# Sixty-eight elementwise instructions of a three-layer network move from GpSimd to VectorE

## The chip, the cores and the metric

The kernel runs on one core of one Trainium2 chip. A core has a matrix engine (TensorE, PE in the profile; its weight loads are PEld), and three engines for elementwise work: VectorE (DVE), ScalarE (ACT) and GpSimd (POOL). SyncE (SP) only issues DMAs here. Each engine works off its own queue of instructions in order and waits for the others by semaphores. The metric is device time in microseconds (us); lower is better.

## What the kernel must compute

The reference takes 256 tokens of width 1024 through three layers, all in float32. Every layer adds a mixer and then a feed-forward part to the residual `x`, each behind an RMS norm whose shift, scale and gate come from a conditioning vector. In its core:

```python
# layer 0: forgetting attention and gated linear attention side by side, then SwiGLU (d_ff 2816)
x = x + g * even_mixer(rmsnorm(x, w) * (1 + sc) + sh, ...)
x = x + g * ((silu(h @ w_gate) * (h @ w_up)) @ w_down)
# layer 1: S5 state space, then a mixture of 8 experts, 2 of them for each token
a = exp(lam_re * dt) * (cos(lam_im * dt) + i sin(lam_im * dt))     # 64 groups x 64 states
y = gelu(C . scan(a, B u) + d_skip * u);  y = (y * sigmoid(y @ w_glu)) @ w_o
x = x + g * sum_e gates[e] * swiglu(h, expert e)
# layer 2: differential attention and RWKV from one input, merged, then PEER
g_a, g_b = split(sigmoid(z_gate))
x = x + g * ((g_a * (o_a @ w_branch_a) + g_b * (o_b @ w_branch_b)) @ w_out)
x = x + g * peer_ffn(...)                                          # 16384 single-row experts
```

## The kernel before

Activations lie transposed on the chip, as eight tiles `x[:, k]` of 128 channels by 256 tokens. Nearly every product is made of float32 operands that are **split** into a high and a low part (`split`, L443 to L447): ScalarE casts the operand to the high part (L445, `...h`), then a subtraction leaves the low part (L446, `...l`), and TensorE forms high x high, low x high and high x low (L421, L422, L423). Weights stream in from HBM: `wpair` (L454 on) loads a block on SP's queue (`w<-...`, L462) and splits it in pieces of 128x512 (`w2882h`, `w2882l` and so on). The block's buffer is free for SP's next load only when both halves of the split are done. `split` and `wpair` take an engine for the subtraction; without one it is VectorE.

The rows of `mods` (L317 to L341) are the conditioning of later layers, and are computed in the shade of earlier ones: 1 MB blocks `wm` are loaded on GpSimd's queue (L328) into two buffers, multiplied on TensorE (`mod<-wm`, L331), copied (`modrow`, L333), transposed (L336) and added to a bias (L339, L341).

Nobody writes the order of the work by hand. The program is built from Python generators, and a scheduler of the tile framework, which simulates a timeline while it builds, lays down the order on each engine. An edit therefore also shifts neighbours.

The places that matter here, in order of time:

- **S5 tables** (`s5_tables`, run as a generator from `layer0_ffn`). While layer 0's feed-forward part goes through its eleven blocks of 256 hidden columns (`gp0` to `gp10`; `gu` and `ga` are its products), powers of the state matrix are built by doubling. `cmul` (L766 to L773) is six tensor_tensor instructions, for 2, 4, ... up to 128 powers. For the last two doublings it is called with GpSimd:

```python
self.cmul(nc.gpsimd if i > 4 else v, tb[:, :, 0, n:2 * n], tb[:, :, 1, n:2 * n], ...
```

- **S5 stage** (`layer1_mix`): `ms`, the sum of squares of the norm (L379), follows on TensorE when `sq` (L378, ScalarE) has squared `x`; then `h2`, then the products `u`. The step over the states (`L910` to `L932`) has one product, `p4` at L919, on GpSimd before and after.
- **Sums of squares**: `route_begin.part` (L974, for the router), `ctx_norm` (L1321, for the context) and `layer2_mix` (L1383) square eight tiles and add them on GpSimd, seven or six additions each.
- **Experts' input** (`route`, L1059): four pieces of 128x512 are split, `hth` on ScalarE and `htl` on GpSimd, while VectorE works out each token's two experts. The one-hot matrix `oh` (L1098) ends that and releases TensorE's `xs` (L425).
- **Merge** (`merge`, L1910 on): while RWKV's last head pairs still run (`chain`, with `R`, `U`, `UV`, `S`, `Y` at L1743 to L1791), the first branch's weights `w_ba` go through a ring of tiles (`ring0h`, `ring0l`, `ringMA`, ...) with the subtraction on GpSimd, and the gate's half sums 0.5 z + 0.5 (`sigmoid`, L1924, tile `sg`) are made there as well; z is already the tanh.

Of the kernel before, what the change touches and what calls it, by code (L numbers as in the profile page):

```python
# [12 lines left out]
OP = mybir.AluOpType  # L13
# [5 lines left out]
KT = 8  # L19
# [230 lines left out]
class K:  # L250
# [524 lines left out]
    def s5_tables(self, p):  # L775
        nc, tc, A = self.nc, self.tc, self.A
        v = nc.vector
# [32 lines left out]
        with tc.tile_pool(name="s5pre2", bufs=1) as q:  # L810
            bs = q.tile([128, 2, 32, 16], F32, tag="bs", name="bs")
            cs = q.tile([128, 2, 32, 16], F32, name="cs")
            nc.gpsimd.dma_start(bs, A["s5_bs"])
            nc.gpsimd.dma_start(cs, A["s5_cs"])
            dte = q.tile([128, 32], F32, name="dts")
            nc.scalar.activation(dte, self.pvec("s5_dt"), AF.Exp)
            mag, co, si, fr, fi, t0, t1 = self.s5_a(q, self.pvec("s5_lr"), self.pvec("s5_li"), dte, 32, "st")
            v.tensor_mul(self.s5m, mag, mag)

            def bk(a, n=16):  # L820
                return a.rearrange("p (t o) -> p t o", o=1).to_broadcast([128, 32, n])

            b2 = q.tile([128, 2, 32, 16], F32, name="bb2")
            tt = q.tile([128, 32, 64], F32, tag="big", name="tt16")[:, :, :16]
            self.cmul(v, b2[:, 0], b2[:, 1], bk(fr), bk(fi), bs[:, 0], bs[:, 1], tt)
            ar, ai = q.tile([128, 32], F32, name="ar"), q.tile([128, 32], F32, name="ai")
            v.tensor_mul(ar, mag, co)
            v.tensor_mul(ai, mag, si)
            yield
            ca = q.tile([128, 2, 32, 16], F32, tag="bs", name="ca")  # L830
            self.cmul(v, ca[:, 0], ca[:, 1], bk(ar), bk(ai), cs[:, 0], cs[:, 1], tt)
            npar = q.tile([128, 2], F32, name="npar")
            v.tensor_scalar(npar, par64, -1.0, None, op0=OP.mult)
            bx = q.tile([128, 2, 32, 32], F32, tag="big", name="bx")
            for j in range(2):
                for dst, src, m in ((self.s5c[:, 0], cs[:, 0], par64), (self.s5c[:, 1], cs[:, 1], npar), (self.s5c[:, 2], ca[:, 0], par64),
                                    (self.s5c[:, 3], ca[:, 1], npar), (bx[:, 0], b2[:, 0], par64), (bx[:, 1], b2[:, 1], npar)):
                    v.tensor_scalar(dst[:, :, 16 * j:16 * j + 16], src, m[:, j:j + 1], None, op0=OP.mult)
            yield
            self.bank = "m"  # L840
            ps = self.psum("k0")
            for t8 in range(8):
                for r in range(4):
                    i = 4 * t8 + r
                    for m in range(2):
                        nc.tensor.matmul(ps[32 * r:32 * r + 32, 16 * t8:16 * t8 + 16], bx[:, m, i], cs[:, m, i], start=m == 0, stop=m == 1)
            k0 = q.tile([128, 8, 16], F32, name="k0")
            v.tensor_copy(k0, ps[:, :128].rearrange("p (t k) -> p t k", t=8))
            self.bank = "f"
            g16 = self.pvec("grp16")  # L850
            for t8 in range(8):
                v.tensor_mul(self.s5k[:, t8].rearrange("p (g k) -> p g k", g=8), k0[:, t8:t8 + 1].to_broadcast([128, 8, 16]),
                             g16.rearrange("p (g o) -> p g o", o=1).to_broadcast([128, 8, 16]))
            yield

            tb = self.s5t
            pw = q.tile([128, 7, 2, 32], F32, name="pw")
            self.cmul(v, pw[:, 0, 0], pw[:, 0, 1], co, si, co, si, t0)
            for i in range(6):
                self.cmul(v, pw[:, i + 1, 0], pw[:, i + 1, 1], pw[:, i, 0], pw[:, i, 1], pw[:, i, 0], pw[:, i, 1], t0)  # L860
            v.memset(tb[:, :, 0, 0:1], 1.0)
            v.memset(tb[:, :, 1, 0:1], 0.0)
            tmp = q.tile([128, 32, 64], F32, tag="big", name="tmp64")
            for i in range(7):
                n = 1 << i
                self.cmul(nc.gpsimd if i > 4 else v, tb[:, :, 0, n:2 * n], tb[:, :, 1, n:2 * n], tb[:, :, 0, 0:n], tb[:, :, 1, 0:n],
                          bk(pw[:, i, 0], n), bk(pw[:, i, 1], n), tmp[:, :, :n])
                if i > 3:
                    yield
# [83 lines left out]
    def route_begin(self):  # L953

        nc, v, mod = self.nc, self.nc.vector, self.mod
        sc = self.moe_sc = self.modscale("o_norm_ffn", mod[:, 80:88], "sc3")
        rt = self.pvec("router").rearrange("p (k e) -> p k e", k=8)
        rw = self.P.tile([128, KT, 8], F32, name="rw")
        v.tensor_mul(rw, rt, sc.rearrange("p (k o) -> p k o", o=1).to_broadcast([128, KT, 8]))
        ps = self.psum("rc")  # L960
        for k in range(KT):
            nc.tensor.matmul(ps[:, :8], mod[:, 72 + k:73 + k].to_broadcast([128, 128]), rt[:, k], start=k == 0, stop=k == KT - 1)
        rc = self.P.tile([128, 8], F32, name="rc")
        v.tensor_copy(rc, ps[:, :8])
        ps = self.psum("lg")
        xt = [[self.psum("xt") for _ in range(2)] for _ in range(2)]
        self.routed = ps, xt, rc
        sqs = []

        def part(k):  # L970
            sq = self.nt.tile([128, T], F32, tag="sq", name=f"rsq{k}", bufs=4)
            nc.scalar.activation(sq, self.x[:, k], AF.Square)
            if 0 < k < 7:
                nc.gpsimd.tensor_add(sq, sq, sqs[-1])  # L974
            sqs.append(sq)
            for t in range(2):
                xk = self.x[:, k, 128 * t:128 * t + 128]
                nc.tensor.matmul(ps[:, 16 * t:16 * t + 8], xk, rw[:, k], start=k + t == 0, stop=k == KT - 1, skip_group_check=True)
                if k >= 6:
                    nc.tensor.matmul(ps[:, 16 * t + 8:16 * t + 9], sq[:, 128 * t:128 * t + 128], self.ones_d[:, 0:1], start=False, stop=k == KT - 1, skip_group_check=True)  # L980
                nc.tensor.transpose(xt[t][k // 4][:, 128 * (k % 4):128 * (k % 4) + 128], xk, self.ident)

        return part

    def route(self, p, q, sc, sh, ht):
# [67 lines left out]
        for t in range(2):  # L1053
            for j in range(2):
                xp = xt[t][j]
                o = ht[:, t, 512 * j:512 * j + 512]
                hn = q.tile([128, 512], F32, name=f"hn{t}{j}")
                nc.scalar.activation(hn, xp, AF.Copy, scale=rs[:, t])
                self.split(hn, o, nc.gpsimd)  # L1059
        for t in range(2):  # L1060
            x, o = xf[:, t], sel[:, t]
            v.tensor_sub(x[:, 8:9], mx[:, t, 1:2], mx[:, t, 0:1])
# [239 lines left out]
    def ctx_norm(self):  # L1302
# [14 lines left out]
        for k in range(KT):  # L1317
            t = load(k, "a")
            nc.scalar.activation(t, t, AF.Square)
            if k:  # L1320
                nc.gpsimd.tensor_add(t, t, before)  # L1321
            before = t
        nc.tensor.matmul(ps[:, :T], self.ones_d, t, start=True, stop=True)
        r = self.rstd(ps[:, :T])
# [17 lines left out]
    def layer2_mix(self):  # L1342
        nc, tc, A, mod = self.nc, self.tc, self.A, self.mod
        m2 = mod[:, 96:144]
        with ExitStack() as c:
# [11 lines left out]
            with ExitStack() as c2:  # L1357
# [3 lines left out]
                with ExitStack() as c3:  # L1361
# [14 lines left out]
                    for k in range(KT):  # L1376
                        a = sq[:, KT + k % 2]
                        if k < 2:
                            v.tensor_scalar(a, sq[:, k], gs[:, 0, k:k + 1], None, op0=OP.mult)
                        else:  # L1380
                            v.scalar_tensor_tensor(a, sq[:, k], gs[:, 0, k:k + 1], a, op0=OP.mult, op1=OP.add)
                        if k:
                            nc.gpsimd.tensor_add(sq[:, KT + 2], sq[:, k], sq[:, KT + 2 if k > 1 else 0])  # L1383
                    for j in range(2):
                        nc.tensor.matmul(ps[0][:, :T], self.ones_d, sq[:, KT + j], start=j == 0, stop=j == 1)
                    self.scaled(self.x, self.rstd(ps[0][:, :T], eps=gs[:, 2, 0:1]), gs[:, 1], m2[:, 0:8], h2[:, :, T:])
# [523 lines left out]
    def merge(self, c, sz, oa, ob, h2, gate, chain):  # L1910
# [10 lines left out]

        def sigmoid(i):
            t = load(sz, i, "sg")
            nc.gpsimd.tensor_scalar(t, t, 0.5, 0.5, op0=OP.mult, op1=OP.add)  # L1924
            return t


# [13 lines left out]
        for b, wo in enumerate((A["w_ba"], A["w_bb"])):  # L1941
            for s in range(4):
                self.bank = "d" if b == 0 else ("a", "d", "ki")[s % 3]
                ws = self.wpair(wo[s], nc.gpsimd if b == 0 else None)
                for i, ps in enumerate(self.wT2("br", ws, h2[:, :, T * b:T * b + T]), 2 * s):
                    sg = sigmoid(KT * b + i)
                    v.tensor_mul(sg, ps[:, :T], sg)
                    if b == 0:
                        nc.sync.dma_start(ma[:, i], sg)
                    else:  # L1950
                        v.tensor_add(sg, sg, load(ma, i, "ma"))
                        self.split(sg, h2[:, i, :T])
# [287 lines left out]
```

## Time and profile before

| | |
|---|---|
| time, median of 3 runs | 3490.37 us (3477.37 to 3495.87) |
| the profiled execution | 3489.14 us, its span 3487.4 us |
| PE, PEld busy | 3207.4 us, 2648.6 us |
| DVE busy | 2309.6 us in 4717 instructions |
| ACT busy | 1710.9 us in 3107 |
| POOL busy | 467.2 us in 478 |

The profiled execution stands 1.7 us above its span and 1.2 us below the median. Busy time is summed over the whole span. "Granted clock" (PEclk) is the share of TensorE's full speed in a stretch. In a row of a timeline the first number is the start, the second how long it took (of several in a row: from the start of the first to the end of the last), and the brackets at the end tell how long the engine had idled before it and what ended that.

### The profile page before, as it was taken

What the parts mean: (1) busy time and instruction counts of PE and PEld (TensorE: products, weight loads), DVE (VectorE), ACT (ScalarE), POOL (GpSimd) and SP (SyncE); (2) the same over time, 40 slices, a digit from 0 to 9 for tenths busy, and PEclk for the clock granted to TensorE, in tenths of its full rate; (3) what the DMA queues carried; (4) which work ended last, traced back from release to release, by engine and by line L of the source; (5) the groups of instructions that cost most, each with busy time, mean ns of one, the idle gap of its engine ahead of it and who ended that gap; (6) DMA issues with size and microseconds to landing.
All of it is one profiled execution on the core that took longest, in us unless ns stands there. A gap on an engine that the chain in (4) does not pass through costs nothing. (4 is left out here: it accounts for less than half of the span.)

```text
span 3487.4 us, 67773 instructions
## 1 busy us (share of the span) xinstructions
PE 3207.4 (92%) x26800; PEld 2648.6 (76%) x26800; DVE 2309.6 (66%) x4717; ACT 1710.9 (49%) x3107; POOL 467.2 (13%) x478
## 2 busy tenths in 40 slices
PE   6989979989999999978899999899879989999999
PEld 4869967766668888746677677667779989988888
DVE  3568858753449999746766666566357767756665
ACT  4445423442226666514544544454436658755554
POOL 0000232200000000010000000000208853410000
PEclk8999988889999999988989888889789999999999
DMA  7666574478798999962111111111435545566775
GB/s 291 237 225 229 200 255 147 125 282 319 321 372 327 337 338 339 356 264 78 45 31 45 45 45 40 45 44 47 141 123 191 159 141 173 176 197 202 231 228 163
DMA packets 162435, 658.51 MB, mean 189 GB/s; under 512 B 18216, under 2 KB 37304, under 8 KB 118208
## 3 DMA queue, kind: packets, MB, share of 16 engines
q1 hardware_dynamic: 145344, 572.33, 46.6%
q0 software_dynamic: 16768, 81.80, 6.9%
q8 instruction: 212, 3.47, 0.4%
q14 instruction: 111, 0.91, 0.1%
HBM read 634.26 MB, written 19.79 MB: 188 GB/s over the span
## 5 line engine op out<-in xcount | busy, mean ns | idle before, releaser
L428 PE MATMUL mg<-mg,xs 128*64 128x256 f32 x1408 | 185.0, 386 | 3.7 <-ACT xf L1101 3.7
L1248 ACT ACTIVATE msg<-mg 128x128 f32<-128x128 f32 (+1 forms) x154 | 42.1, 273 | 260.3 <-PE mg L428 191.2
L428 PEld LDWEIGHTS mg<-mg,xs 128*64 128x64 f32 x1408 | 106.2, 138 | 68.1 <-issue 15.8
L331 PE MATMUL mod<-wm,c 128*32 128x256 f32 x1152 | 100.2, 452 | 50.0 <-DMA wm<-mods 45.5
L1363 POOL DMA_DIRECT2D h2h<-hch x1 | 1.0, 960 | 821.6 <-DVE squares L1372 821.6
L331 PEld LDWEIGHTS mod<-wm,c 128*32 128x32 f32 x1152 | 37.7, 123 | 87.7 <-DMA wm<-mods 44.4
L1814 POOL MEMSET X<- 128x272 f32 x8 | 3.0, 378 | 753.6 <-DVE UV L1754 217.9
L1249 DVE TENSOR_TENSOR msg<-msg,mg 128x128 f32<-128x128 f32 (+1 forms) x154 | 43.4, 282 | 76.4 <-ACT msg L1248 75.9
L328 POOL DMA_DIRECT2D wm<-mods x64 | 34.6, 541 | 386.2 <-PE mod L331 374.5
L2024 POOL TENSOR_SCALAR oh<-iota,idx 128x128 f32<-128x128 f32 x44 | 58.3, 1324 | 146.1 <-PE G L2034 146.1
L2027 ACT ACTIVATE oh<-oh,idx 128x128 f32<-128x128 f32 x212 | 69.1, 393 | 6.4 <-DVE oh L2019 6.4
L2019 DVE TENSOR_TENSOR oh<-iota,idx 128x1024 f32<-128x1024 f32 x53 | 67.6, 1278 | 0.0
L2034 PE MATMUL G<-oh 128*128 128x128 f32 x512 | 62.5, 275 | 0.0
L1152 DVE COPY mgt<-mg 128x128 f32<-128x128 f32 x44 | 12.8, 290 | 75.0 <-PE mg L1145 74.8
L367 DVE RECIPROCAL rs<-rs 128x512 f32<-128x512 f32 (+1 forms) x16 | 44.0, 2752 | 27.7 <-ACT rs L366 27.6
L2034 PEld LDWEIGHTS G<-oh 128*128 128x128 f32 x512 | 60.1, 192 | 0.0
L428 PE MATMUL ya<-md,mgt 128*64 128x512 f32 x176 | 55.1, 604 | 4.2 <-DVE mgt L1152 4.0
L2067 POOL DMA_DIRECT2D a<-ad x32 | 17.3, 542 | 284.9 <-DVE ap48l L446 127.1
L428 PE MATMUL yb<-md,mgt 128*64 128x512 f32 x176 | 54.0, 592 | 0.0
L2039 ACT COPY Gate<-G 128x288 f32<-128x288 f32 x64 | 43.3, 678 | 20.4 <-DVE acts L2038 20.4
L1760 PEld LDWEIGHTS S<-UV,BKt 128*64 128x64 f32 x448 | 22.3, 150 | 37.3 <-issue 13.8
L928 PE MATMUL y<-st,s5c 128*32 128x128 f32 x256 | 43.7, 320 | 6.5 <-DVE st L920 6.5
(11890 smaller groups left out, 12677.0 us busy)
## 6 DMA issues: line engine op xcount, KB each, us to landing
mg<-m_gu SPq DMA_DIRECT2D x176, 1024.0 KB, 7.8
md<-m_dn SPq DMA_DIRECT2D x88, 1024.0 KB, 8.0
wm<-mods POOLq DMA_DIRECT2D x64, 1024.0 KB, 6.1
w<-u SPq DMA_DIRECT2D x128, 512.0 KB, 3.7
w<-v SPq DMA_DIRECT2D x128, 512.0 KB, 4.2
w<-w_in SPq DMA_DIRECT2D x132, 256.0 KB, 2.7
w<-e_gu SPq DMA_DIRECT2D x44, 512.0 KB, 4.4
w<-e_in SPq DMA_DIRECT2D x24, 512.0 KB, 4.8
```

Of the source, the lines that this page charges most:

```text
L328: (nc.gpsimd if later else nc.sync).dma_start(ws, self.A["mods"][g, kp].rearrange("p j k c -> p (j k) c"))
L331: nc.tensor.matmul(ps[32 * j:32 * j + 32, :256], c[:, 2 * kp + k, :], ws[:, 2 * j + k, :], start=kp + k == 0, stop=kp + k == 4)
L367: nc.vector.reciprocal(t[:, :n], t[:, :n])
L428: mm(ps, w, h, start=start, stop=stop, **kw)
L928: nc.tensor.matmul(py[o, 128 * j:128 * j + 128], self.s5c[:, ci + m, i0 + r], st[:, r, m, off:off + 128], start=False, stop=m == 1, skip_g ...
L1248: nc.scalar.activation(sg[:rows], ps[:rows, :128], AF.Silu)
L1249: v.tensor_mul(sg[:rows], sg[:rows], ps[:rows, 128:256])
L2019: v_.tensor_tensor(o, iota.rearrange("p (a b i) -> p a b i", a=1, b=1).to_broadcast([128, 2, 4, 128]), idx[:, 0:2, 4 * t4:4 * t4 + 4].rear ...
L2024: nc.gpsimd.tensor_scalar(o[:, 0, t], iota, i1, w, op0=OP.is_equal, op1=OP.mult)
L2027: nc.scalar.activation(o[:, 0, t], o[:, 0, t], AF.Copy, scale=w)
L2034: nc.tensor.matmul(ps[:, 128 * t:128 * t + 128], o[:, 1, t], o[:, 0, t], start=True, stop=True)
L2039: nc.scalar.copy(G[0][:, :, ts].rearrange("p i t -> p t i"), pv[:, :, HF:120])
```

## The change

Seven calls lose their GpSimd argument or engine. Every instruction stays, with the same operands; 68 of them change their engine: 12 of the tables, 6 + 7 + 7 additions of squares, 4 subtractions of the experts' input, 16 subtractions and 16 half sums of the merge.

```diff
@@ s5_tables
-                self.cmul(nc.gpsimd if i > 4 else v, tb[:, :, 0, n:2 * n], tb[:, :, 1, n:2 * n], tb[:, :, 0, 0:n], tb[:, :, 1, 0:n],
+                self.cmul(v, tb[:, :, 0, n:2 * n], tb[:, :, 1, n:2 * n], tb[:, :, 0, 0:n], tb[:, :, 1, 0:n],
@@ route_begin.part
-                nc.gpsimd.tensor_add(sq, sq, sqs[-1])
+                nc.vector.tensor_add(sq, sq, sqs[-1])
@@ route
-                self.split(hn, o, nc.gpsimd)
+                self.split(hn, o)
@@ ctx_norm
-                nc.gpsimd.tensor_add(t, t, before)
+                nc.vector.tensor_add(t, t, before)
@@ layer2_mix
-                            nc.gpsimd.tensor_add(sq[:, KT + 2], sq[:, k], sq[:, KT + 2 if k > 1 else 0])
+                            v.tensor_add(sq[:, KT + 2], sq[:, k], sq[:, KT + 2 if k > 1 else 0])
@@ merge.sigmoid
-            nc.gpsimd.tensor_scalar(t, t, 0.5, 0.5, op0=OP.mult, op1=OP.add)
+            v.tensor_scalar(t, t, 0.5, 0.5, op0=OP.mult, op1=OP.add)
@@ merge
-                ws = self.wpair(wo[s], nc.gpsimd if b == 0 else None)
+                ws = self.wpair(wo[s])
```

On VectorE, in layer 0's feed-forward part around `gp8`, the table products (`s5t`, `tmp`) now stand among the splits of the weights (`w2872l` and so on, 128x512 each) and of the hidden columns (`gp8l`); `g` is the gated product:

```order
 L446 TENSOR_TENSOR w2880l<-w_4783,w2880h 128x512
+L770 TENSOR_TENSOR s5t<-s5t,tmp_4622 128x32x32
 L446 TENSOR_TENSOR w2882l<-w_4783,w2882h 128x512
 L446 TENSOR_TENSOR w2910l<-w_4851,w2910h 128x512
+L725 TENSOR_TENSOR g_4700<-gu_4721,sg_4770 128x256
+L772 TENSOR_TENSOR tmp_4622<-s5t,pw 128x32x32
+L768 TENSOR_TENSOR s5t<-s5t,pw 128x32x64
+L771 TENSOR_TENSOR s5t<-s5t,pw 128x32x64
 L446 TENSOR_TENSOR w2911l<-w_4851,w2911h 128x512
 L446 TENSOR_TENSOR w2920l<-w_4861,w2920h 128x512
-L725 TENSOR_TENSOR g_4700<-gu_4721,sg_4770 128x256
 L446 TENSOR_TENSOR gp8l<-g_4700,gp8h 128x256
```

Three products of 1024 and 2048 columns now lie between the splits, and `g` moves up ahead of them. In all, the twelve table instructions are spread from `gp7` to `gp9`.

On TensorE, behind layer 0's feed-forward part and ahead of the S5 stage, `mod<-wm` matmuls (a row for each 1 MB block `wm`) stand between the last `ga`, the norm's `ms` and the first `u`:

```order
 L423 MATMUL ga_2253<-gp10h,w3221l 128x256
-L331 MATMUL mod_5197<-wm_5208,c_90 32x256 x8
-L331 MATMUL mod_5197<-wm_5218,c_90 32x256 x8
 L331 MATMUL mod_5197<-wm_5228,c_90 32x256 x8
 L336 MATMUL mod_5197<-c_ident,modrow_5238 128x128 x2
-L331 MATMUL mod_6064<-wm_6065,c_90 32x256 x8
 L379 MATMUL ms_5496<-sq_0_5497,ones_d 128x256
 L379 MATMUL ms_5496<-sq_1_5500,ones_d 128x256
 L379 MATMUL ms_5496<-sq_2_5503,ones_d 128x256
 L379 MATMUL ms_5496<-sq_3_5506,ones_d 128x256
-L331 MATMUL mod_6064<-wm_6075,c_90 32x256 x8
+L331 MATMUL mod_6064<-wm_6065,c_90 32x256 x8
```

Of the seven blocks that stood between the last `ga` and the first `u`, four are left (`wm_5228`, `wm_6065`, `wm_6075`, `wm_6085`); `wm_5208` and `wm_5218` stand earlier, among `gu` and `ga`, and `wm_6095` with its `modrow` stands later, in the S5 stage's loop.

On ScalarE, in the merge, the casts of the ring and RWKV's `UV` of the last step of a head pair (`U_25329`) change places:

```order
 L445 CAST ring1h<-w_26623 128x512
+L445 CAST ring2h<-w_26627 128x512
+L445 CAST ring3h<-w_26631 128x512
 L1753 ACTIVATE UV_25103<-U_25329 64x128
-L445 CAST ring2h<-w_26627 128x512
 L1777 COPY y_25102<-Y_25336 128x2x64
 L1896 ACTIVATE TT_25458<-p_25611 16x16x16 x2
-L445 CAST ring3h<-w_26631 128x512
```

`UV` stood ahead of two casts that wait for a load, and now stands behind both.

## Rows read from the trace of the kernel before

**Rows 1.** The page: busy time of each engine, and one costly group.

```profile
PE 3207.4 (92%) x26800; PEld 2648.6 (76%) x26800; DVE 2309.6 (66%) x4717; ACT 1710.9 (49%) x3107; POOL 467.2 (13%) x478
...
L2019 DVE TENSOR_TENSOR oh<-iota,idx 128x1024 f32<-128x1024 f32 x53 | 67.6, 1278 | 0.0
```

**Rows 2.** Stretches: length, then busy time (instructions) of each engine, granted clock, DMA.

```profile
400.00:416.00 16.00, 16.00 (x162) 13.51 (x162) 14.72 (x45) 5.14 (x10) 2.11 (x4) 1.00 0.79 278
416.00:474.00 58.00, 41.88 (x344) 37.65 (x342) 48.46 (x36) 16.41 (x31) 40.54 (x16) 0.88 0.59 202
484.00:505.00 21.00, 21.00 (x201) 18.48 (x197) 11.69 (x26) 8.87 (x17) 2.11 (x4) 1.00 0.92 327
505.00:532.00 27.00, 16.01 (x130) 7.67 (x122) 6.33 (x13) 7.39 (x16) 3.17 (x6) 0.71 0.81 287
541.00:550.00 9.00, 8.91 (x75) 8.71 (x74) 4.45 (x6) 6.41 (x18) 4.12 (x7) 1.00 0.69 213
690.00:715.00 25.00, 24.13 (x204) 23.68 (x203) 9.15 (x18) 7.72 (x16) 4.62 (x6) 0.98 0.14 32
```

**Rows 3.** TensorE's waits from 416 to 480 us.

```profile
PE ga L421 <- ACT gp8h L445: 8.3, 1, 8.3
PE ga L422 <- DVE gp8l L446: 3.3, 1, 3.3
```

**Rows 4.** Timeline of GpSimd in the tables.

```profile
429.91 4.07 POOL L768 TENSOR_TENSOR s5t<-s5t,pw 128x2048 f32<-128x2048 f32 x1
...
437.96 0.60 POOL L328 DMA_DIRECT2D wm<-mods  x1
```

**Rows 5.** Timeline of VectorE ahead of the tables and in them.

```profile
405.83 0.42 DVE L771 TENSOR_TENSOR s5t<-s5t,pw 128x256 f32<-128x256 f32 x1
...
415.04 0.69 DVE L446 TENSOR_TENSOR w2832l<-w,w2832h 128x512 fp32r<-128x512 f32 x1
...
416.57 2.30 DVE L446 TENSOR_TENSOR w2840l<-w,w2840h 128x512 fp32r<-128x512 f32 x1
...
430.42 4.11 DVE L446 TENSOR_TENSOR w2882l<-w,w2882h 128x512 fp32r<-128x512 f32 x1
...
469.71 3.89 DVE L446 TENSOR_TENSOR gp9l<-g,gp9h 128x256 fp32r<-128x256 f32 x1 [0.47 <-ACT gp9h L445]
```

**Rows 6.** Timeline of TensorE, last of ScalarE, between feed-forward part and S5 stage.

```profile
504.82 1.07 PE L331 MATMUL mod<-wm,c 128*32 128x256 f32 x16
509.51 1.80 PE L331 MATMUL mod<-wm,c 128*32 128x256 f32 x16 [3.62 <-DMA wm<-mods]
...
530.38 1.93 PE L331 MATMUL mod<-wm,c 128*32 128x256 f32 x16 [2.47 <-DMA wm<-mods]
...
517.09 1.33 ACT L378 ACTIVATE sq<-xT 128x256 f32<-128x256 f32 x4 [11.62 <-PE mod L336]
```

**Rows 7.** The router: TensorE's wait, then the timelines of GpSimd and VectorE.

```profile
PE xs L425 <- DVE oh L1098: 8.9, 1, 8.9
...
719.80 3.71 POOL L446 TENSOR_TENSOR htl<-hn,hth 128x512 fp32r<-128x512 f32 x3 [0.85 <-ACT hth L445]
...
719.86 1.23 DVE L1066 TENSOR_TENSOR tok<-xf,tok 128x1 f32<-128x1 f32 x1
722.23 0.15 DVE L1066 TENSOR_TENSOR tok<-xf,tok 128x1 f32<-128x1 f32 x1
```

**Rows 8.** Timeline of VectorE in the squares of layer 2.

```profile
1547.00 4.48 DVE L1381 SCALAR_TENSOR_TENSOR squares<-squares,gains 128x256 f32<-128x256 f32 x5
1552.55 0.86 DVE L446 TENSOR_TENSOR w16000l<-w,w16000h 128x512 fp32r<-128x512 f32 x1 [1.07 <-ACT w16000h L445]
```

**Rows 9.** The merge: timelines of ScalarE, then of GpSimd.

```profile
2481.78 0.27 ACT L1753 ACTIVATE UV<-U 64x128 f32<-64x128 f32 x1
...
2488.00 0.62 ACT L445 CAST ring3h<-w 128x512 fp32r<-128x512 f32 x1 [2.14 <-DMA w<-w_ba]
...
2530.23 0.61 POOL L1924 TENSOR_SCALAR sg<-sg 128x256 f32<-128x256 f32 x1 [8.30 <-DMA sg<-sz]
```

## The prediction

> **What bounds the kernel now.** I read the page first. TensorE is busy 3207.4 of 3487.4 us and VectorE 2309.6 [rows 1], so all of TensorE's idle time is 280 us, spread over many stages. No engine total decides this change; it is worth what TensorE waits, or runs slowly, in the seven places where GpSimd loses work. So I cut those places out of the span with stretches of busy time, asked there for TensorE's waits, and followed the largest back through the timelines.
>
> Only one place is large. From 416 to 474 us, where GpSimd computes the last two doublings of the S5 tables, TensorE runs 344 matmuls in 58.0 us; in the 16 us before it runs 162 in 16.0 [rows 2]. [...] The two largest waits are 8.3 us for the high part of `gp8`, which is cast late because `g` stood in VectorE's queue, and 3.3 us for its low part [rows 3].
>
> Why is VectorE late? GpSimd's 2048-column product starts at 429.91 and ends at 433.98 [rows 4]. VectorE's split of 128x512 starts at 430.42 and is shown to take 4.11 us; the same split ahead of the tables takes 0.69 [rows 5]. 430.42 + 4.11 = 434.53, which is 0.55 after GpSimd's end: the split does its work when GpSimd has finished. Twelve VectorE instructions in the stretch look like this, from the one at 416.57 (2.30) to the one at 469.71 (3.89) [rows 5]; together 37.5 us where the free durations, 0.69 at 512 columns and 0.42 at 256, make 7.5. GpSimd's tables thus cost VectorE 30.0 of its 48.46 busy us [rows 2].
>
> **The tables, -15.** Taken out of GpSimd, they give VectorE 30.0 us back. Added to VectorE are six products of 1024 and six of 2048 columns. Between 256 and 512 columns a product grows from 0.42 to 0.69 [rows 5], 0.00105 us a column, so 0.69 + 512 x 0.00105 = 1.23 at 1024, which agrees with 1.278 for another product of 1024 [rows 1], and 2.31 at 2048: 6 x 1.23 + 6 x 2.31 = 21.2. VectorE's need is then 48.5 - 30.0 + 21.2 = 39.7 us, more than TensorE's 34.0: VectorE becomes the bound of this stretch. Its queue is in order and had 92% busy at 400 to 416 (14.72 of 16) [rows 2]; at that density 39.7 takes 43, and 58 - 43 = 15. Bounds: 58 - 39.7 = 18.3 with no gap; and 3.3 if only TensorE's long wait for a low part goes [rows 3] while `g` stays late.
>
> [...]
>
> **The conditioning blocks, -6.** GpSimd's queue also issues the `wm` loads, and one stood behind the tables: it goes out at 437.96, the moment the product ahead of it ends, without idle time [rows 4]. With the tables gone the scheduler consumes `wm` earlier. Before, seven blocks stand between the last `ga` and the first `u`; from the first at 504.82 to the last at 530.38 they take 25.6 us, 4.26 a block, waiting for DMA [rows 6]. The squares of the norm wait behind the third of them, 11.62 us [rows 6]. Afterwards four blocks stand there: three fewer are 12.8 us. But these bytes must move earlier, when DMA is already 0.92 busy with 327 GB/s at 484 to 505; from 416 to 474 it moved 202 GB/s x 58 us = 11.7 MB [rows 2]. In 43 us that is 272 GB/s, which leaves (327 - 272) x 43 = 2.4 MB, some two blocks. Half the 12.8 is my value, bounds 0 and -12.8. What is late next is DMA itself.
>
> **The S5 loop, +1.** The fourth displaced thing, `wm_6095`'s `modrow` and its additions, now runs in the state loop on VectorE: one copy of 256 columns (0.42 at most, [rows 5]) and small additions; 0.5 to 1.5. One `wm` load also moves behind the first `p4` products in GpSimd's queue, where the next `p4` waits with it for TensorE; I count it in this.
>
> **The context's and the router's squares, 0.** 7 and 6 additions of 256 columns, 0.42 each, put 2.9 and 2.5 us on VectorE. It is busy 4.45 of 9.0 us in the one stretch and 9.15 of 25 in the other, while TensorE is at 8.91 of 9.0 and 24.13 of 25 with other products [rows 2]. That cover hides them; without it they would cost the 5.4.
>
> **The experts' input, -1.** Here VectorE's chain to `oh` holds TensorE for 8.9 us. Three of the four GpSimd splits lie in 719.80 to 723.51, and a product of one column takes 1.23 us under them where its twin takes 0.15 [rows 7]. Four such instructions lose 4 x 1.08 = 4.3 us. On VectorE the four splits cost 4 x 0.69 = 2.8, some of it while it waits for the casts. Net -1.5 at best, 0 if casts come late; -1.
>
> **Layer 2's squares, 0.** Under GpSimd's additions five products take 4.48 us, 0.90 each, and then VectorE idles 1.07 for a cast whose weights are late [rows 8]. Seven additions at 0.34 to 0.42 fit in what the products save and in that gap: -0.5 to +2.
>
> **The merge, +1.** 16 splits of 0.69 and 16 half sums of about 0.3 go to VectorE, 16 us spread over some 130. SP's weight loads come free sooner. Against that, ScalarE now does `UV` behind the cast of `ring3h`. `UV` ran at 2481.78, that cast at 2488.00 [rows 9]; if the load lands no sooner, RWKV's chain is late by 6.8 us. But 1 MB (`xT<-xd`) that SP issued ahead of that load now goes behind it. The half sums wait for `sg` loads in VectorE's queue, the longest shown 8.30 [rows 9], with RWKV's `S` steps behind. +1, bounds -3 and +7. Other reordering, mainly at the start of layer 2, I hold at 0 +- 3.
>
> **Sum.** -15 - 6 + 1 - 1 + 1 = -20. On the profiled execution's 3489.14 that is 3469. That execution is 1.2 below the median of the runs shown, so the gain against the median is 21, or 0.6%; 0.5%, about what can be told from no change here, is 17.
>
> **Rivals.**
> - *DMA takes back what the tables give.* The table stretch cannot shrink as far if `wm` and the weights come no faster, and the four blocks left are waited for longer. For it: 0.92 and 0.81 busy around [rows 2]. Against: 0.59 in the stretch itself. The tables then give 9 or 10 and the blocks nothing: 3480.
> - *Both terms at their upper bounds.* VectorE without gaps and all three blocks ahead: -18.3 - 12.8 and -1 for the rest, 3457.
> - *VectorE's queue becomes as bad as GpSimd's.* Table products of 2.3 us stand ahead of `gp8l`, and `g` is late again. Only the 3.3 go: 3486. Against it: a split is held for 2.3 at worst and not for 3.4, and `g` moved up in the new order.
> - *Slower: loads hold RWKV's chain in the merge.* `UV` waits for `ring3h` (6.8), and VectorE stands three times for `sg` as long as GpSimd did the one time shown (8.30) [rows 9]: 31.7 in all, in place of my +1: 3500. It decides from 21 us of such holds on. Against it: most `sg` loads are issued well before use, and matmuls of `br` lie under the rest.
> - *Slower: the long splits are not GpSimd's doing.* If their 2 to 4 us come from something that stays, the 21.2 us of table products are added to a full queue: 3510. It decides if more than half of the 30.0 us stays. Against it: the ends that follow GpSimd's ends by 0.55.
>
> **How the numbers follow.** The forecast 0.45 (its own range 3462 to 3477), DMA 0.20, upper bounds 0.12, queue 0.10, merge 0.08, splits 0.05. 3454 to 3490 holds all but the last two. Faster by over 0.5% is below 3473: four fifths of the forecast and the upper bounds, some 0.5. Slower: 0.05 and a tail of the merge, 0.06. The rest, 0.44, within 0.5%.
>
> **What would show it.** Splits of 0.69 and table products of 1.2 and 2.3 in VectorE's timeline around 430 us, and 344 matmuls in about 43 us, show the first term; no such shortening falsifies it. The first `u`, right behind the block at 530.38 [rows 6], should come near 511; near 520, with each of the four blocks waited for, means DMA. `UV` within 2 us of the cast of `ring1h` means the merge holds nothing. The forecast is wrong if VectorE is full in the stretch and TensorE's waits for `gp8` and `gp9` stay above 8 us, or if the stretch from 2460 to 2600 grows by over 7.

## The result and the profile after

The changed kernel takes 3455.24 us (median of 8 runs, 3441.97 to 3467.48); the kernel before, run beside it, 3488.67 (8 runs, 3468.81 to 3500.55). The ratio is 0.9908 [0.9885, 0.9931]: 33 us faster, where 20 were forecast. The profiled execution's span is 3453.4 us, 34.0 less than before.

The page's busy line answers to [rows 1].

```profile
PE 3199.9 (93%) x26800; PEld 2641.7 (76%) x26800; DVE 2305.1 (67%) x4785; ACT 1712.4 (50%) x3107; POOL 381.7 (11%) x410
```

GpSimd loses 68 instructions and 85.5 us. VectorE gains the 68, and is busy 4.5 us less: what it no longer stands waiting for under GpSimd outweighs the work it took over.

To find the place, I cut every span at the same instructions. The start is VectorE's sum of 128x512 (L770) just ahead of the tables; stage A goes from there to the last `ga`, B to the first `u`, C to the first `p4`, D to the router's `xs`, E to RWKV's first `R`, F to its last `R`, G to the end. Each number is a difference of two starts in the timelines (us).

| kernel | start | A | B | C | D | E | F | G |
|---|---|---|---|---|---|---|---|---|
| before | 415.6 | 89.0 | 27.6 | 27.9 | 167.6 | 892.0 | 938.2 | 929.5 |
| after | 412.8 | 71.5 | 15.5 | 27.9 | 165.0 | 893.1 | 937.5 | 930.0 |
| difference | -2.8 | -17.5 | -12.1 | 0 | -2.6 | +1.1 | -0.7 | +0.5 |

A and B give 29.6 of the 34.0. Each row is one profiled execution. The start is no effect of the edit: among kernels that run the same instructions up to there it varied from 412.8 to 420.8, so a difference of a few us in one stage need not be the edit's either.

Stage A, in stretches of the changed kernel. As in [rows 2]: length, then busy time (instructions) of PE, PEld, DVE, ACT and POOL, granted clock, DMA share, GB/s. The last row is the whole stage.

```profile
412.81:452.00 39.19, 39.19 (x366) 35.07 (x365) 37.88 (x49) 15.58 (x29) 3.43 (x7) 1.00 0.85 307
452.00:471.00 19.00, 18.88 (x178) 17.07 (x180) 10.70 (x23) 8.32 (x15) 1.24 (x5) 1.00 0.94 341
...
412.81:484.30 71.49, 71.37 (x664) 63.59 (x663) 55.43 (x84) 29.24 (x54) 6.26 (x15) 1.00 0.89 320
```

The same stage in the kernel before:

```profile
415.64:504.60 88.96, 72.84 (x632) 65.03 (x631) 65.54 (x72) 28.94 (x54) 43.65 (x25) 0.92 0.68 234
```

TensorE is now busy for 71.37 of 71.49 us, with the clock at 1.00 throughout; before, 16.1 us were idle and the clock averaged 0.92. The stage now holds 32 matmuls more: two `mod` blocks that came forward from B, at 1.07 us each (the length of such a row in stage B below). Without them it would take 71.49 - 2.1 = 69.4, so of the 88.96 of before 19.6 us were lost. All of that is back, the two blocks cost 2.1, and 19.6 - 2.1 = 17.5.

VectorE's timeline in the tables answers to [rows 5].

```profile
424.19 0.68 DVE L446 TENSOR_TENSOR w2910l<-w,w2910h 128x512 fp32r<-128x512 f32 x1
425.12 1.22 DVE L772 TENSOR_TENSOR tmp<-s5t,pw 128x1024 f32<-128x1024 f32 x1
426.25 2.28 DVE L768 TENSOR_TENSOR s5t<-s5t,pw 128x2048 f32<-128x2048 f32 x1
428.46 2.28 DVE L771 TENSOR_TENSOR s5t<-s5t,pw 128x2048 f32<-128x2048 f32 x1
430.66 0.68 DVE L446 TENSOR_TENSOR w2911l<-w,w2911h 128x512 fp32r<-128x512 f32 x1
431.86 0.42 DVE L446 TENSOR_TENSOR gp8l<-g,gp8h 128x256 fp32r<-128x256 f32 x1
...
452.16 0.42 DVE L446 TENSOR_TENSOR gp9l<-g,gp9h 128x256 fp32r<-128x256 f32 x1
```

No split is held: 0.68 at 512 columns and 0.42 at 256, where [rows 5] have up to 4.11 and 3.89. A table product is shown with 1.22 at 1024 columns and 2.28 at 2048 (1.23 and 2.31 were worked out). From the start of the stage to the end of `gp9l` it is 39.8 us now and was 58.0 [rows 5], and these 18.2 us are all of A's gain of 17.5. TensorE's two longest waits from 416 to 505 us, which answer to [rows 3]:

```profile
PE mod L331 <- DMA wm<-mods: 2.4, 1, 2.4
PE mod L336 <- DVE modrow L333: 2.1, 1, 2.1
```

Both lie behind the last `ga`, in stage B; the waits for `gp8` are gone. Stage B on TensorE, for [rows 6]:

```profile
484.54 1.07 PE L331 MATMUL mod<-wm,c 128*32 128x256 f32 x16
487.66 0.44 PE L336 MATMUL mod<-c_ident,modrow 128*128 128x128 f32 x2 [2.06 <-DVE modrow L333]
488.61 3.38 PE L379 MATMUL ms<-sq,ones_d 128*128 128x256 f32 x8 [0.51 <-ACT sq L378]
491.92 1.31 PE L331 MATMUL mod<-wm,c 128*32 128x256 f32 x16
495.09 1.07 PE L331 MATMUL mod<-wm,c 128*32 128x256 f32 x16
498.61 1.32 PE L331 MATMUL mod<-wm,c 128*32 128x256 f32 x16 [2.45 <-DMA wm<-mods]
499.85 0.58 PE L421 MATMUL u<-h2h,w3260h 128*128 128x256 f32 x1
```

Four blocks and one wait for a load stand there; the first `u` starts at 499.85, where 511 was forecast.

### The profile page after: what moved, and what is told of

Read it like the earlier page. It is cut to its first block, busy times and chain, and to the rows that moved or that the text cites. A ratio compares the mean times of both kernels' runs of the same rounds, so it can differ in the third digit from the quotient of the medians.

```text
span 3453.4 us, 67721 instructions
## 1 busy us (share of the span) xinstructions
PE 3199.9 (93%) x26800; PEld 2641.7 (76%) x26800; DVE 2305.1 (67%) x4785; ACT 1712.4 (50%) x3107; POOL 381.7 (11%) x410
## 5 line engine op out<-in xcount | busy, mean ns | idle before, releaser
L1152 DVE COPY mgt<-mg 128x128 f32<-128x128 f32 x44 | 12.8, 290 | 76.2 <-PE mg L1145 76.0
L367 DVE RECIPROCAL rs<-rs 128x512 f32<-128x512 f32 (+1 forms) x16 | 44.0, 2752 | 23.0 <-ACT rs L366 22.9
L1760 PE MATMUL S<-UV,BKt 128*64 128x64 f32 x448 | 35.5, 257 | 12.8 <-ACT UV L1753 7.7
```

Source lines behind the costliest of these rows:

```text
L367: nc.vector.reciprocal(t[:, :n], t[:, :n])
L1760: nc.tensor.matmul(ps[dh[o], 64 * d:64 * d + 64], BKt[:, d, c, dh[o]], UV[:, js[d], dh[o]], start=True, stop=True)
```

## The experiments

Eight kernels, in the order in which they ran. e1 to e4 ask what gives the gain, e5 to e8 by what GpSimd holds VectorE (a held instruction is one shown far longer than its free duration), and why a half-way version loses. The column "total" is the ratio to the kernel before, run beside each; the stages are those of one profiled execution.

| kernel | median us | total | start | A | B | C | D | E | F | G |
|---|---|---|---|---|---|---|---|---|---|---|
| e1 | 3450.51 | 0.9890 [0.9863, 0.9917] | 420.8 | 72.3 | 15.4 | 28.6 | 166.2 | 895.5 | 933.2 | 924.0 |
| e2 | 3487.35 | 0.9996 [0.9981, 1.0011] | 419.3 | 88.9 | 27.3 | 27.2 | 170.8 | 894.0 | 936.2 | 925.3 |
| e3 | 3481.44 | 0.9976 [0.9957, 0.9996] | 419.3 | 82.7 | 13.0 | 31.9 | 174.0 | 893.8 | 947.3 | 924.0 |
| e4 | 3501.95 | 1.0040 [1.0022, 1.0058] | 416.9 | 93.5 | 13.4 | 30.4 | 183.7 | 892.2 | 952.3 | 923.5 |
| e5 | 3514.45 | 1.0078 [1.0054, 1.0102] | 414.8 | 87.2 | 23.9 | 28.4 | 169.5 | 892.4 | 970.2 | 932.0 |
| e6 | 3478.47 | 0.9981 [0.9961, 1.0002] | 437.7 | 74.8 | 12.6 | 28.8 | 162.6 | 893.9 | 935.5 | 931.9 |
| e7 | 3452.55 | 0.9910 [0.9887, 0.9933] | 415.0 | 74.7 | 14.4 | 28.6 | 162.6 | 890.7 | 926.2 | 930.9 |
| e8 | 3491.83 | 1.0012 [0.9988, 1.0035] | 419.9 | 86.9 | 23.8 | 28.2 | 166.9 | 892.2 | 950.6 | 923.6 |

**e1: the tables alone.** The kernel before with one of the seven edits:

```diff
-                self.cmul(nc.gpsimd if i > 4 else v, tb[:, :, 0, n:2 * n], ...
+                self.cmul(v, tb[:, :, 0, n:2 * n], ...
```

> Only the tables' twelve products go to VectorE; the other six edits are undone. Theory A (GpSimd's products held VectorE's splits, and the conditioning blocks were consumed earlier once the tables left GpSimd's queue): 3455 to 3460 us, the stretch of the tables about 17 shorter and the stretch from the last ga to the first u about 12 shorter than before. Theory B (the other edits carry a third or more of the gain): about 3467 us or more.

It is as fast as the whole change, and A and B are the same within 0.8 us: Theory A. The tables bring all of the gain.

**e2: all but the tables.** The other six edits, with the line above as before.

> The six other edits, the tables left on GpSimd. Theory A: within 4 us of the kernel before, the long splits of 2 to 4 us still there, seven conditioning blocks between ga and u, 27 us. Theory B: 10 us or more below it.

No gain and no loss beyond 0.2%. TensorE's two longest waits in the tables are those of [rows 3], to the tenth:

```profile
PE ga L421 <- ACT gp8h L445: 8.3, 1, 8.3
PE ga L422 <- DVE gp8l L446: 3.3, 1, 3.3
```

Fifty-six of the 68 instructions thus move for nothing measurable.

**e3: the tables twice.** The changed kernel, which computes each of the last two doublings a second time on VectorE, some 21.2 us of work added and the same values:

```diff
+                if i > 4:
+                    self.cmul(v, tb[:, :, 0, n:2 * n], ...
```

> As the changed kernel, but the last two doublings are computed twice on VectorE, 21 us more of its work, in the blocks gp7 to gp10. Theory A with TensorE as the bound of the changed stretch: 0 to 6 us above the changed kernel, TensorE still full. Theory C (VectorE is the bound, as in my sum): 15 to 21 us above it, 3470 or more.

It is 31 us above e1 and 26 above the changed kernel, more than either theory gave, and neither explains it. Stage A in stretches, with the last rows of VectorE's timeline that count there:

```profile
419.00:485.00 66.00, 65.19 (x608) 58.56 (x608) 64.05 (x82) 26.70 (x49) 5.84 (x11) 1.00 0.82 298
485.00:502.00 17.00, 10.79 (x78) 7.98 (x77) 10.72 (x17) 2.71 (x6) 1.24 (x5) 0.70 0.87 326
419.28:502.00 82.72, 75.70 (x681) 66.26 (x680) 74.48 (x98) 29.41 (x54) 6.80 (x16) 0.94 0.83 304
...
493.52 2.28 DVE L773 TENSOR_TENSOR s5t<-s5t,tmp 128x2048 f32<-128x2048 f32 x1
495.72 0.42 DVE L446 TENSOR_TENSOR gp10l<-g,gp10h 128x256 fp32r<-128x256 f32 x1
```

VectorE does 74.48 us in this stage, 19 more than in the changed kernel. Up to 485 it is busy 97% of the time, and TensorE still is busy for 65.19 of 66.00 us at full clock. All that TensorE waits for in the stage is this:

```profile
PE mod L331 <- DMA wm<-mods: 6.9, 3, 4.5
```

So up to 485 not even twice the table work makes VectorE the engine that TensorE waits for. A grows by 11.2 behind that: one more `mod` block stands in it, its loads are waited for, and the clock is 0.70 around those waits. That VectorE has no part in this is not shown: the second half of `gp10l` is split at 495.72, behind the last table product, and ends 1.5 us before TensorE is through with the `mod` blocks ahead (497.6), so without the waits for loads TensorE might have waited for it instead. The rest is in D (+9.0), F (+9.8) and C (+4.0), where the edit adds no instruction; one `mod` block moved from D to C. In D the state loop of the S5 stage runs its first 50 us at a granted clock of 0.52 here, and then of 0.80 in the changed kernel:

```profile
546.80:596.80 50.00, 50.00 (x241) 35.91 (x241) 39.96 (x143) 2.47 (x6) 12.49 (x22) 0.52 0.03 7
```

```profile
527.80:577.80 50.00, 47.99 (x349) 35.37 (x349) 46.24 (x168) 2.47 (x6) 16.37 (x30) 0.80 0.23 75
```

Why the clock stayed low there, and what made C and F longer, is open.

**e4: the late loads off GpSimd's queue.** The kernel before, with the `wm` loads of four groups of `mods` issued on SP's queue:

```diff
-                (nc.gpsimd if later else nc.sync).dma_start(ws, ...
+                (nc.gpsimd if later and not 11 < g < 16 else nc.sync).dma_start(ws, ...
```

> As the kernel before, tables on GpSimd, but the conditioning blocks of four groups are loaded on SP's queue, so they do not stand behind the tables; the scheduler then leaves three blocks between the last ga and the first u in place of seven. Theory A: the tables' stretch stays 58 us with the long splits, the stretch from ga to u shrinks by 8 to 12, 3477 to 3483 us in all. Theory D (the blocks came earlier only because the tables' stretch was shorter): the blocks are waited for elsewhere and the time is that of before, or above it if SP's weight loads are held.

B falls by 14.2, to three blocks, without any change to the tables. So what stands in B is a matter of when the loads are issued. But A rises by 4.5: it holds three blocks more (680 matmuls for 632), and TensorE waits for held splits as before. All of A and its longest wait:

```profile
416.87:510.37 93.50, 77.91 (x680) 66.96 (x679) 67.14 (x73) 28.90 (x54) 39.57 (x15) 0.93 0.73 254
...
PE ga L421 <- ACT gp8h L445: 6.8, 1, 6.8
```

D rises by 16.1 and F by 14.1, and the kernel is slower. In D, the state loop of the S5 stage:

```profile
544.00:554.00 10.00, 10.00 (x92) 9.62 (x90) 7.39 (x14) 7.69 (x15) 1.49 (x2) 1.00 0.78 245
554.00:574.00 20.00, 20.00 (x87) 14.47 (x87) 16.95 (x63) 0.82 (x2) 5.58 (x9) 0.51 0.06 23
```

and in the kernel before:

```profile
560.00:580.00 20.00, 20.00 (x123) 14.83 (x122) 19.73 (x73) 0.82 (x2) 6.38 (x11) 0.74 0.04 18
```

TensorE was busy at 1.00 up to 554, then the granted clock is 0.51 for the loop, where it was 0.74 before: 87 matmuls in 20 us where 123 ran. The trace does not show why it fell here for longer. Theory A, which had the blocks' gain arrive in the total, did not hold; the total is as in Theory D, with the time lost in later stages.

**e5: the last doubling on GpSimd.** The changed kernel with the second of the two doublings put back:

```diff
-                self.cmul(v, tb[:, :, 0, n:2 * n], ...
+                self.cmul(nc.gpsimd if i > 5 else v, tb[:, :, 0, n:2 * n], ...
```

> The changed kernel, but the last doubling (six products of 2048 columns, 24.8 of GpSimd's 38 us) is computed on GpSimd. Six conditioning blocks then stand between the last ga and the first u. Theory A (hold by GpSimd's products, and the blocks): the stretch from the tables to the last ga gives back half or more of its 17.5 us, the stretch from ga to u 6 to 9 of its 12; 18 to 22 us above the changed kernel. Theory C (VectorE's own work is the limit): 13.9 us less VectorE work, so faster than the changed kernel in that stretch.

A and B rise by 24.1 together, a little above what was expected; Theory C, by which A was to shrink, fails. The held splits are back; VectorE's timeline, then GpSimd's:

```profile
438.01 4.11 DVE L446 TENSOR_TENSOR w2980l<-w,w2980h 128x512 fp32r<-128x512 f32 x1
442.04 5.00 DVE L446 TENSOR_TENSOR w2982l<-w,w2982h 128x512 fp32r<-128x512 f32 x1
...
437.57 4.00 POOL L769 TENSOR_TENSOR tmp<-s5t,pw 128x2048 f32<-128x2048 f32 x1 [2.77 <-DVE s5t L773]
441.64 4.84 POOL L770 TENSOR_TENSOR s5t<-s5t,tmp 128x2048 f32<-128x2048 f32 x1
```

The splits end at 442.12 and 447.04, GpSimd's products at 441.57 and 446.48: 0.55 and 0.56 later, as in the kernel before. But the median is 59 us above the changed kernel's, because F, in layer 2, is 32.7 longer, which no theory had; e8 takes that up.

**e6 and e7: unused work on GpSimd, reading and writing.** The changed kernel, in which GpSimd does work whose result nobody uses. The scheduler placed it ahead of the tables, from 341 or 342 us on: in e6 52 products of 128x256, which read two operands in SBUF, the engines' on-chip memory, in e7 128 fills of 128x256, which read none.

```diff
+            dum = q.tile([128, 16, 16], F32, name="dum64")
+            v.tensor_mul(dum, cs[:, 0, :16], cs[:, 1, :16])
...
+                if i > 4:
+                    for _ in range(26):
+                        nc.gpsimd.tensor_mul(dum, cs[:, 0, :16], cs[:, 1, :16])
```

e7 has the same tile `dum`, and then:

```diff
+                if i > 4:
+                    for _ in range(64):
+                        nc.gpsimd.memset(dum, 0.0)
```

> The changed kernel plus 52 products of 256 columns on GpSimd that nobody uses (both operands and the result in SBUF, some 0.74 us each, 38 us in all), which run around gp3 to gp5, where VectorE is 0.9 busy. Theory A: VectorE's two-operand instructions under them take up to 0.7 longer each, TensorE waits for splits there, 10 to 25 us above the changed kernel. Theory E (the long splits came from waiting for the tables' results, not from GpSimd's work as such): no VectorE instruction gets longer, only the wm loads behind are late, under 5 us.

> The same place, but the unused GpSimd work only writes: 128 memsets of 256 columns, some 30 to 40 us in all. If it is the reading that holds VectorE, its instructions keep 0.42 and 0.69, and the time is that of the changed kernel but for late wm loads, under 5 us above. If any work of GpSimd holds VectorE: as with the products, 10 to 25 above.

The start of A comes 22.6 us later in e6 than in e7, and the medians are 25.9 apart; e6 is 23 above the changed kernel, and e7 is as fast as it. The stretch with the unused work, e6 and then e7:

```profile
342.00:399.00 57.00, 41.63 (x300) 39.06 (x301) 56.97 (x84) 16.38 (x31) 52.64 (x52) 0.90 0.35 108
```

```profile
341.00:389.00 48.00, 47.66 (x402) 47.01 (x403) 42.37 (x119) 21.93 (x41) 40.77 (x127) 0.96 0.55 173
```

GpSimd is busy 92% of the one and 85% of the other. Under the reads VectorE is full and does 84 instructions in 57 us; under the fills it does 119 in 48, and TensorE is busy for 47.66 of them. Under the reads TensorE is idle for 15.4 us; its two longest waits are for held splits:

```profile
PE gu L423 <- DVE w2370l L446: 2.7, 1, 2.7
PE ga L422 <- DVE gp5l L446: 2.2, 1, 2.2
```

The timeline of VectorE shows the same two lines of code, in e6 and then in e7:

```profile
360.22 1.22 DVE L446 TENSOR_TENSOR w2310l<-w,w2310h 128x512 fp32r<-128x512 f32 x1
361.36 0.41 DVE L725 TENSOR_TENSOR g<-gu,sg 128x256 f32<-128x256 f32 x1
362.49 0.73 DVE L773 TENSOR_TENSOR pw<-pw,st_t 128x32 f32<-128x32 f32 x1
```

```profile
352.15 0.68 DVE L446 TENSOR_TENSOR w2310l<-w,w2310h 128x512 fp32r<-128x512 f32 x1
353.68 0.18 DVE L773 TENSOR_TENSOR pw<-pw,st_t 128x32 f32<-128x32 f32 x1
```

A split is held to 1.22 from 0.68, a tiny product to 0.73 from 0.18; `g`, one of whose operands (`gu`) lies in the matmuls' accumulators, keeps its 0.41. So GpSimd's products hold VectorE though nobody needs their results, and its fills do not; the two kinds differ in that the one reads operands and the other only writes.

**e8: the last doubling alone.** The kernel before, and of the whole change only the first of the two doublings moved to VectorE:

```diff
-                self.cmul(nc.gpsimd if i > 4 else v, tb[:, :, 0, n:2 * n], ...
+                self.cmul(nc.gpsimd if i > 5 else v, tb[:, :, 0, n:2 * n], ...
```

> The kernel before with one edit: the doubling to 64 powers goes to VectorE, the last one stays on GpSimd, and the other six edits are undone. In the stretches ahead of the state space stage it should repeat the earlier kernel with the last doubling on GpSimd: about 87 us from the tables' start to the last ga. In that kernel RWKV's stage of layer 2, 1100 us later and with no edit in it that the changed kernel lacks, took 970 us where the others take 926 to 952. Theory F (the scheduler happened to lay a slow order there): another order here, 926 to 952 again, and 3465 to 3490 in all. Theory G (a doubling left on GpSimd slows the late stage by itself): 970 again, 3510.

A and B are those of e5 within 0.3 us, with the same table work on GpSimd, but F is 950.6 and not 970.2. The long F of e5 thus does not come with the doubling alone. That speaks for Theory F, the order that the scheduler lays down in layer 2: VectorE's 1286 instructions in F are the same ones in e5 and in the changed kernel, but at 1114 places of their order a different one stands. That the doubling and the other six edits do it only together is not excluded. Stage F in e5, in the changed kernel and in e8:

```profile
1616.00:2587.00 971.00, 875.42 (x10019) 682.36 (x10019) 592.11 (x1286) 428.49 (x794) 4.21 (x14) 0.86 0.18 54
```

```profile
1586.00:2524.00 938.00, 864.05 (x10016) 672.10 (x10017) 591.45 (x1286) 431.61 (x796) 4.17 (x14) 0.88 0.18 56
```

```profile
1618.00:2569.00 951.00, 867.61 (x10016) 675.14 (x10016) 589.73 (x1259) 432.05 (x797) 30.34 (x41) 0.87 0.18 55
```

TensorE's instructions are the same but for a few records; its idle time (95.6, 74.0 and 83.4 us) and its granted clock (0.86, 0.88 and 0.87) differ. Which row begins it was not found. No version tried is faster than the changed kernel by more than the intervals.

## Why the prediction came out as it did

The time lies inside the range of 3454 to 3490, 1.2 us from its lower end, but outside the forecast's own 3462 to 3477. The cause of the gain was named rightly, and so was the place. The likeliest size was too small in both large terms. The total is that of the rival "both terms at their upper bounds" (3457, chance 0.12); its reason came true only in part, since VectorE is without gaps but nothing waits for it, and one of the three blocks did not come ahead. That the time fell inside the range owes more to its width than to the sum.

- **The tables: -15 forecast, -19.6 measured.** The cause was read rightly: the splits are free, and e5 brings the holds back. VectorE's need was about right too: 39.7 us were worked out, and in the first 39.19 us of the stage, in which the twelve table products run almost to the end of the last (452.24), it was busy 37.88 (97%). The step that failed is "VectorE becomes the bound of this stretch", with its 92% density: 344 matmuls were to take 43 us. TensorE did 366 in those 39.19 us and waited for nothing, so an engine at 97% did not hold it. TensorE's 34.0 us, which VectorE's need is set against, were off as well, and no run shows them: they are 344 matmuls at the pace of 400 to 416 us, 162 in 16.0 [rows 2], and that pace counts short matmuls of `mod` as full ones. Those alone, in the kernel before, with PE and PEld:

```profile
400.00:416.00 16.00, 4.08 (x64) 1.77 (x64) 1.00 0.79 278
416.00:474.00 58.00, 4.69 (x64) 1.89 (x64) 0.88 0.59 202
```

  Apart from them 98 matmuls took 11.92 us, 0.1216 each, so the 344 need 280 x 0.1216 + 4.08 = 38.1 and not 34.0, and 58.0 - 38.1 = 19.9 us were lost there. TensorE and VectorE thus need nearly the same.
- **The blocks: -6 forecast, -10.0 measured,** that is -12.1 in B less the 2.1 that two of them cost in A. Four blocks are left, as the order said, and B's length for each block is as before (15.5 / 4 = 3.9, 27.6 / 7 = 3.9). The 327 GB/s of [rows 2], which I took as DMA's limit by estimate (341 were moved at 452 to 471 us of the changed kernel), gave two blocks that could come forward, and two did: A moved 320 GB/s over 71.49 us, 22.9 MB against 234 x 88.96 = 20.8 before. The step that failed is "Half the 12.8 is my value": the third block did not have to come earlier. It went into D, at no loss that can be seen, so B lost all three. e4 shows the same fall of B from the loads alone, but there the total gained nothing.
- **The S5 loop: +1 forecast.** C is unchanged and D 2.6 shorter, while D varies by 4 us among kernels whose tables all run once on VectorE (162.6 in e7, 166.2 in e1). A term of 1 us can't be seen in it.
- **The squares, 0,** and **the experts' input, -1.** e2 holds them all and is 0.9996. In the router the split is free and the product of one column back at 0.15, but TensorE's wait for `oh` goes only from 8.9 [rows 7] to 8.2, 0.7 of the 1 us forecast; the wait, then two rows of VectorE's timeline:

```profile
PE xs L425 <- DVE oh L1098: 8.2, 1, 8.2
...
683.44 0.69 DVE L446 TENSOR_TENSOR htl<-hn,hth 128x512 fp32r<-128x512 f32 x1
687.88 0.15 DVE L1066 TENSOR_TENSOR tok<-xf,tok 128x1 f32<-128x1 f32 x1
```

- **The merge: +1 forecast, F -0.7 and G +0.5 measured.** ScalarE's timeline, for [rows 9]:

```profile
2445.78 0.62 ACT L445 CAST ring1h<-w 128x512 fp32r<-128x512 f32 x1 [1.75 <-DMA w<-w_ba]
...
2447.45 0.62 ACT L445 CAST ring3h<-w 128x512 fp32r<-128x512 f32 x1
2448.88 0.27 ACT L1753 ACTIVATE UV<-U 64x128 f32<-64x128 f32 x1 [0.82 <-PE U L1752]
```

  `ring3h` is cast 1.67 us after `ring1h`, where [rows 9] let one expect a load to wait for; `UV` starts 3.1 us after `ring1h`, past the 2 that the prediction set, but it waits for TensorE's `U` and not for a cast. No cast holds `UV`, and neither stage with the merge in it grew by more than 0.5 us, so the slower rival did not happen.
- **The rivals.** DMA took nothing back: one wait for `wm` of 2.4 us is left in B, where [rows 6] have waits of 3.62 and 2.47 among others. VectorE's queue is not as bad as GpSimd's: no wait for `gp8` or `gp9`. The long splits were GpSimd's doing: e5 and e6.

## What to carry to other kernels

When one engine's instructions take several times their free duration, look at which instruction of another engine ends just ahead of each of them: here GpSimd's products ended 0.55 and 0.56 us ahead of the ends of the splits (e5). The price of work on a helper engine can stand in a neighbour's queue. An engine that is 97% busy does not yet bound a stretch: see whether another engine waits for it, and take the other's need from matmuls of the same kind, since a pace over a mixture misled here by 4 us. Compare versions stage by stage, since a stage far from an edit can change by as much as the edit is worth (F, 937.5 to 970.2 us in e5, whose median confirms it).

## What the runs showed of the hardware

The rows behind the prediction had only GpSimd products; the runs add that its fills do not hold VectorE: the same split took 1.22 us under products and 0.68 under fills (e6, e7). 52 products put the start of A 22.6 us later than 128 fills did, with GpSimd busy 92% and 85% of the stretch. `g`, with one operand outside SBUF, took 0.41 under the products and 0.42 under the fills; no run moves that operand alone, so whether its place spares `g` was not shown. The time added was not larger for a larger held instruction: under products of 256 columns one of 32 columns goes from 0.18 to 0.73 us and one of 512 from 0.68 to 1.22, 0.55 and 0.54 more. It was larger under larger products of GpSimd: under those of 2048 columns the splits of 512 took 4.11 and 5.00 and ended 0.55 and 0.56 after them (e5).
